# HGRN2 with keys taken into the exponential as logarithms, and a Newton step in two operations

## The chip, the core and the metric

One core of one Trainium2 chip runs the whole program. The metric is device time in microseconds (us), the median of the runs shown. The engines are TensorE (PE in the profile, with its weight loads as PEld), VectorE (DVE), ScalarE (ACT), GpSimd (POOL) and SyncE (SP), which issues most of the DMAs.

## The reference

A trunk of one layer on 1024 tokens of width 1024 in float32: a SwiGLU feed-forward part, a mixer of three branches (S5, HGRN2, RG-LRU), a second SwiGLU part and a final norm. The change concerns the second branch, which has four heads of 128 key and 128 value channels and works in chunks of 64 tokens:

```
qh = silu(q);  log_f = log(lb + (1 - lb) * sigmoid(zf));  kh = (1 - lb) * sigmoid(-zf)
# for each chunk, with the state from the chunk before
b = cumsum(log_f)
o_inter = (qc * exp(b)) @ state
scores[t, s] = sum_d qc[t, d] * exp(b[t, d] - b[s, d]) * kc[s, d]      for s <= t
o = o_inter + scores @ vc
state = exp(b_last) * state + (kc * exp(b_last - b)).T @ vc
# after the chunks, per head
out = o * rsqrt(mean(o * o) + 1e-6) * norm_w * silu(g)
```

## The kernel before

The products with weights, which are most of the work, run on TensorE in float32 by three passes over exact halves (`mm3`, lines 207 to 209). The mixers' elementwise work runs on the other engines beside them. `w_in` projects all columns; `pbuf_out` applies each column's first function, and for the f columns computes the key `k = (1 - lb) * sigmoid(-z)` on the way (lines 1501 to 1505); all goes to scratch in DRAM.

HGRN2 comes afterwards, in eight halves: four heads `j`, two halves `hf` of the tokens (512 columns). `run` (lines 1705 to 1708) calls `hgrn` for one half and then a few steps of the generator `fill`: the merges of the branches (`merge`: product, evacuation `th` on VectorE in line 1549, sums on GpSimd in line 1554) and the first half of the output product. The table `FILL` says how many steps. What an engine runs in which order is set by a list scheduler when the program is built; each engine's queue is then fixed and runs in order.

One half (`hgrn_half`), with channels on the partitions and tokens on the columns:

- A logarithm on ScalarE (line 1021) and a scan on VectorE (line 1024) give `b`, the running sum of log f in each chunk of 64. Two exponentials give `E = exp(b)` and `Ek = exp(b_last - b)`, whose difference GpSimd takes (lines 1027 to 1029).
- Level 64: VectorE multiplies queries with `E` and keys with `Ek` (lines 1035 to 1040) into `QK`, `Qin` and `Kh`. All elementwise products here go through the helper in line 1020, so the trace tells them apart by their tiles only.
- Six levels of block size H = 32 to 1 (lines 1057 to 1076). In each, GpSimd subtracts a reference from `b` for the two halves of the blocks into `Dl`, ScalarE takes the exponential in place, VectorE multiplies the key half with `k` and the query half with `q` (256 columns each), TensorE forms four 128 x 128 score products (line 1051), and VectorE copies them by mask into `sc`.
- The keys are transposed, the state is advanced, the outputs are summed in `po` (lines 1078 to 1102).
- The head norm: the sum of squares in `pm` by a product with ones (line 1106), then `rsqrt` (lines 223 to 235): logarithm and exponential on ScalarE and one Newton step of five operations on VectorE. Then `y` with the norm weight (line 1109), times the gate `g` on GpSimd.

Tiles of a half live in one of two tags, `h` with nine and `h2` with eight slots, for even and odd heads; a slot comes free when its last reader is done. `b`, `sc`, `Qin` and `Kh` keep theirs through the levels, `Dl` takes a new one in each level.

Of the kernel before, what the change touches and what calls it, by code (L numbers as in the profile page):

```python
# [11 lines left out]
ALU = mybir.AluOpType  # L12
# [27 lines left out]
def pack(inp):  # L40
    """small parameters, channel-major on 128 partitions (layout only)"""
# [20 lines left out]
class Trunk:  # L62
# [3 lines left out]
    COPIES = 3      # of four rounded on DVE  # L66
# [22 lines left out]
    def open_psum(self, **kinds):  # L89
        """eight banks in sets"""  # L90
        self.banks.close()
        self.pp = self.banks.enter_context(self.tc.tile_pool(name=self.nm("pp"), bufs=1, space=PSUM, reuse_waits="tile"))
        self.kinds = kinds

    def ps(self, kind="g"):
        """one PSUM bank of a set"""
        return self.pp.tile([P, HALF], F32, name=self.nm("ps"), tag="ps" + kind, bufs=self.kinds[kind])
# [4 lines left out]
    def open_pool(self, ctx, side="right", **bufs):  # L102
        """tags of equal slots; the tiles of one tag share its slots in program order"""
# [8 lines left out]
    # ---- constants  # L112
    def consts(self):
# [9 lines left out]
        nc.scalar.activation(out=warm, in_=self.epsb, func=AF.Sqrt)      # the table of the first norm  # L123
# [7 lines left out]
    # ---- weight stream: raw float32 tiles ahead of their exact hi/lo halves  # L131
    def add_unit(self, src, k, c=P, kind="n"):
        """src: AP [128, k, c], k * c <= 1024"""
        self.units.append((src, k, c, kind))

    def add_cols(self, w, c0, k0=0, k=KD, c=P, kind="n"):
        """rows [k0*128, (k0+k)*128) and columns [c0, c0+c) of w"""
# [22 lines left out]
    def _split_unit(self, i):  # L160
# [13 lines left out]
        if kind == "u":  # L174
            # weight sums of the seven products: A11, A12 from g, A21, A22 from u
# [13 lines left out]
    def after_unit(self, ahead):  # L189
        """queue the block's loads behind the load of the weights `ahead` units from here"""  # L190
# [11 lines left out]
    def mm3(self, ps, pairs, start=True, stop=True):  # L202
        """ps += sum of l.T @ r over the pairs, float32 by three passes over exact halves"""
# [18 lines left out]
    # ---- 1/sqrt(v) for v = scale * a + eps, polished by one Newton step  # L222
    def rsqrt(self, a, scale, table=None):
        nc = self.nc
        ln, v, r = (self.slot("t") for _ in range(3))
        b = nc.scalar.activation(out=ln, in_=a, func=AF.Ln, scale=scale, bias=self.epsb)
        if table is not None:
            self.order(b, table)
        nc.vector.tensor_scalar(out=v, in0=a, scalar1=scale, scalar2=EPS, op0=ALU.mult, op1=ALU.add)
        nc.scalar.activation(out=r, in_=ln, func=AF.Exp, scale=-0.5)  # L230
        nc.vector.tensor_tensor(out=ln, in0=r, in1=r, op=ALU.mult)
        nc.vector.tensor_tensor(out=v, in0=v, in1=ln, op=ALU.mult)
        nc.vector.tensor_scalar(out=v, in0=v, scalar1=-0.5, scalar2=1.5, op0=ALU.mult, op1=ALU.add)
        nc.vector.tensor_tensor(out=r, in0=r, in1=v, op=ALU.mult)
        return r

    def rsqrt_small(self, o, a, scale):
        """o = 1/sqrt(scale * a + eps) for a few values a partition"""
# [12 lines left out]
    def act_set(self, sid, after):  # L251
        """ask for an activation-table set once `after` have been issued"""
# [10 lines left out]
    # ---- the residual stream, tokens on partitions: tile (g, cq) holds tokens 256 g.. and columns 256 cq.. as [128, 2, 256]  # L263
# [3 lines left out]
    def stats(self, hf):  # L267
        """columns for the sums of squares of one half of the tokens: [128, 4 tiles, 4 parts]"""
# [8 lines left out]
    def inv_rms(self, sq, i0=0, i1=4, n=4):  # L277
        """1 / rms of the token tiles [i0, i1)"""
# [24 lines left out]
    # ---- FFN, first part: silu(h @ gate) * (h @ up), to scratch  # L303
    # The gate and up columns of one tile are the two rows of a 2 x 2 block product with the halves of the inner
    # dimension and of the tokens: seven block products in place of eight.
    def t_open(self, ctx):
        """slots for the halves of the seven blocks, before that for the tiles they come from"""
# [11 lines left out]
    def t_blocks(self, src, n, names, parts=1):  # L319
        """w * x of one half of the tokens, transposed, in float32 and as halves, in parts of the tokens;  # L320
        src(i, d): normed x [128 tokens, 128 columns]"""
# [16 lines left out]
    def t_second(self, src, n):  # L338
        """B12 serves only the tiles done in eight products"""
# [32 lines left out]
    def tiles8(self, hf, w, parts=1):  # L372
        """the first tiles of gate and up columns in eight products, a half of the tokens"""
# [24 lines left out]
    def tick(self):  # L398
        """work beside the products: one job is done and the loads of the next begin, every so many products"""
# [7 lines left out]
    def pair7(self, out, early=False):  # L407
        """two column tiles of a product with h, by seven products; out(column tile, half, its value)"""
# [10 lines left out]
        tt(g1, g0, p6)                                  # P1 + P6  # L419
        if not early:  # L420
            p2 = prod("g", w, 4, "21")
        tt(g0, g0, p2)                                  # P1 + P2
# [4 lines left out]
        tt(u0, g1, p7)                                  # P1 + P6 + P7  # L427
        tt(g1, g1, p5)                                  # P1 + P6 + P5
# [11 lines left out]
    def tile7(self, f, sums=False):  # L440
# [9 lines left out]
        tt(g1, g0, p6)                                  # P1 + P6  # L450
        p2 = prod("g", w, 4, "21")
        tt(g0, g0, p2)                                  # gate, first half: P1 + P2
# [4 lines left out]
        tt(u0, g1, p7)                                  # P1 + P6 + P7  # L457
# [1316 lines left out]
```

## Time and profile before

| | us |
|---|---|
| median of three runs | 2341.26 (2340.84 to 2343.86) |
| span of the profiled execution, first to last instruction | 2343.5 |
| run time nearest to that span | 2343.86 |
| TensorE busy | 2270.5 (97%) |
| TensorE weight loads busy | 1902.2 (81%) |
| VectorE busy | 1803.5 (77%) |
| ScalarE busy | 940.8 (40%) |
| GpSimd busy | 248.0 (11%) |

The profiled execution's own time is not marked among the runs; the nearest, 2343.86 us, is 0.36 us above the span. The busy shares are averages over stages with different limits, so they must be read stage by stage. Where the rows below speak of idle time before an instruction, they name the work that ended it. A busy TensorE is not one at its peak, since matmuls are pipelined and their ends are modelled.

### The profile page before, as it was taken

The page shows a single profiled execution, that of the slowest core. Times are in us where ns is not written, and L with a number is a line of the kernel's source. Part 1 is how long each engine was busy: PE and PEld are TensorE (multiplying, and loading weights), DVE is VectorE, ACT ScalarE, POOL GpSimd, SP SyncE. Part 2 cuts the span into 40 slices and gives each one's busy share as a digit, 9 for nine tenths or more (in the row PEclk, how much of TensorE's full clock was granted, in tenths as well). Part 3 has the DMA queues.
Part 4 walks back from the last instruction along what each step waited for, and adds up shares of the span by engine and source line. Part 5 has one row for each costly group of instructions (what it writes and reads, how often), then busy time and mean ns, then how long its engine had stood idle before and what let it go on. Part 6 is the DMA issues. An engine that isn't in the chain of part 4 may idle for free.

```text
span 2343.5 us, 32057 instructions
## 1 busy us (share of the span) xinstructions
PE 2270.5 (97%) x11476; PEld 1902.2 (81%) x11476; DVE 1803.5 (77%) x3179; ACT 940.8 (40%) x1510; POOL 248.0 (11%) x250
## 2 busy tenths in 40 slices
PE   7999999999999999999999998899999999999998
PEld 6788888899789888887778777788978888888887
DVE  6976777698797876667887989986478777775796
ACT  5323222222466523435665533344423222234455
POOL 0100000005200300000000445520020000000000
PEclk9999999999999999999999999999999999999999
DMA  5122433474843446563445543347513433348633
GB/s 154 57 87 86 116 113 121 147 249 122 272 158 124 135 142 202 180 196 108 148 137 148 174 143 125 104 141 228 158 32 119 151 104 117 102 136 288 215 95 117
DMA packets 354255, 336.96 MB, mean 144 GB/s; under 512 B 43920, under 2 KB 258320, under 8 KB 354080
## 3 DMA queue, kind: packets, MB, share of 16 engines
q1 hardware_dynamic: 353920, 334.36, 45.2%
q8 instruction: 90, 1.47, 0.3%
q0 software_dynamic: 176, 0.56, 0.1%
q14 instruction: 69, 0.57, 0.1%
HBM read 233.53 MB, written 102.50 MB: 143 GB/s over the span
## 4 chain that ended last, share of the span: by engine, by line
PE 78%; DVE 12%; DMA 3%; issue 3%; POOL 1%; ACT 1%; SPq 1%; DVEq 0%; ACTq 0%; POOLq 0%
PE ps L208 25%; PE ps L207 25%; PE ps L209 24%; DVE w L157 2%; DVE Dl L1020 1%; DVE th L1549 1%; DVE TT L317 1%; POOL tb L343 1%; PE ps L1051 1%; PE ps L292 1%; DVE S L177 1%; DMA yl<-y 1%; PE ps L905 0%; DVE b L1024 0%; DVE tb L343 0%
## 5 line engine op out<-in xcount | busy, mean ns | idle before, releaser
L208 PE MATMUL ps<-T,w 128*128 128x512 f32 (+1 forms) x992 | 384.2, 388 | 1.4 <-DVE T L317 1.4
L207 PE MATMUL ps<-T,w 128*128 128x512 f32 (+1 forms) x992 | 383.6, 389 | 1.2 <-DVE T L316 1.2
L209 PE MATMUL ps<-T,w 128*128 128x512 f32 (+1 forms) x992 | 380.7, 385 | 0.0
L156 ACT CAST w<-raw 128x1024 fp32r<-128x1024 f32 (+2 forms) x218 | 181.7, 836 | 357.5 <-PE ps L208 309.7
L157 DVE TENSOR_TENSOR w<-raw,w 128x1024 fp32r<-128x1024 f32 (+2 forms) x218 | 212.5, 976 | 66.5 <-ACT w L156 63.5
L156 ACT CAST w<-S 128x1024 fp32r<-128x1024 f32 x128 | 134.3, 1049 | 320.6 <-PE ps L208 318.5
L208 PE MATMUL ps<-TT,w 128*128 128x512 f32 x640 | 254.4, 398 | 7.0 <-DVE TT L317 6.9
L209 PE MATMUL ps<-TT,w 128*128 128x512 f32 x640 | 251.4, 393 | 0.0
L207 PE MATMUL ps<-TT,w 128*128 128x512 f32 x640 | 250.4, 394 | 0.0
L207 PEld LDWEIGHTS ps<-T,w 128*128 128x128 f32 x992 | 186.1, 189 | 43.3 <-DVE T L316 1.9
L208 PEld LDWEIGHTS ps<-T,w 128*128 128x128 f32 x992 | 187.0, 189 | 41.0 <-DVE T L317 2.2
L209 PEld LDWEIGHTS ps<-T,w 128*128 128x128 f32 x992 | 187.0, 189 | 39.3 <-DVE w L157 0.2
L445 DVE TENSOR_TENSOR g<-g,ps 128x512 f32<-128x512 f32 x160 | 109.9, 687 | 116.7 <-PE ps L209 115.6
L157 DVE TENSOR_TENSOR w<-S,w 128x1024 fp32r<-128x1024 f32 x128 | 161.3, 1261 | 22.7 <-ACT w L156 18.4
L208 PEld LDWEIGHTS ps<-TT,w 128*128 128x128 f32 x640 | 120.6, 188 | 38.7 <-DVE TT L317 12.5
L207 PEld LDWEIGHTS ps<-TT,w 128*128 128x128 f32 x640 | 121.0, 189 | 27.9
L208 PE MATMUL ps<-b,ah 128*128 128x512 f32 x360 | 142.3, 396 | 0.0
L209 PEld LDWEIGHTS ps<-TT,w 128*128 128x128 f32 x640 | 120.8, 189 | 26.4
L156 ACT CAST ah<-ar 128x512 fp32r<-128x512 f32 (+2 forms) x153 | 79.9, 524 | 150.8 <-PE ps L208 101.4
L207 PE MATMUL ps<-b,ah 128*128 128x512 f32 x360 | 137.9, 393 | 0.0
L209 PE MATMUL ps<-b,ah 128*128 128x512 f32 x360 | 134.0, 392 | 0.0
L157 DVE TENSOR_TENSOR ah<-ar,ah 128x512 fp32r<-128x512 f32 (+2 forms) x153 | 86.3, 571 | 46.7 <-ACT ah L156 42.9
(408 smaller groups left out, 5041.5 us busy)
## 6 DMA issues: line engine op xcount, KB each, us to landing
raw<-in_w_in_dram SPq DMA_DIRECT2D x56, 512.0 KB
raw<-in_ffn_gate_dram SPq DMA_DIRECT2D x44, 512.0 KB
raw<-in_ffn_up_dram SPq DMA_DIRECT2D x44, 512.0 KB
B<-in_ffn_down_dram SPq DMA_DIRECT2D x68, 256.0 KB
ar<-s SPq DMA_DIRECT2D x68, 256.0 KB
ar<-a SPq DMA_DIRECT2D x66, 256.0 KB
s<-S SPq DMA_DIRECT2D x62, 256.0 KB
a<-a SPq DMA_DIRECT2D x56, 256.0 KB
```

Of the source, the lines that this page charges most:

```text
L156: self.nc.scalar.copy(hi, src)
L157: self.last_lo = self.nc.vector.tensor_tensor(out=lo, in0=src, in1=hi, op=ALU.subtract)
L177: tt = lambda o, a, b, op: nc.vector.tensor_tensor(out=o, in0=a, in1=b, op=op)
L207: nc.tensor.matmul(out=ps, lhsT=lh, rhs=rh, start=start and j == 0, stop=False)
L208: nc.tensor.matmul(out=ps, lhsT=lh, rhs=rl, start=False, stop=False)
L209: self.last_mm = nc.tensor.matmul(out=ps, lhsT=ll, rhs=rh, start=False, stop=stop and j == n - 1)
L292: self.nc.tensor.transpose(ps[:, i * P:(i + 1) * P], src(i), self.ident)
L317: self.nc.vector.tensor_tensor(out=lo[:, c], in0=x[:, c], in1=hi[:, c], op=ALU.subtract)
L343: tt = lambda o, a, b, e=self.nc.vector: e.tensor_tensor(out=o, in0=a, in1=b, op=ALU.subtract)
L445: tt = lambda o, a, b, op=ALU.add: V.tensor_tensor(out=o, in0=a, in1=b, op=op)
L1020: tt = lambda o, a, b, op, e=V: e.tensor_tensor(out=o, in0=a, in1=b, op=op)
L1051: nc.tensor.matmul(out=ps[:, c * P:(c + 1) * P], lhsT=lh[:, c * P:(c + 1) * P], rhs=rh[:, c * P:(c + 1) * P], start=True, stop=True)
```

## The change

Every place where the key was multiplied with an exponential now has the key's logarithm inside that exponential: `c = b - ln k` is formed once per half, and the differences for the key side are taken against `c` in place of `b`, so that `exp(ref - c) = k * exp(ref - b)`. The exponential of `Ek` is written straight to its two users. `k` is held above 1e-37 so that its logarithm exists. The Newton step of the head norm uses `r * (r * r * (pm + P * eps) - 3 P)`, two fused operations on VectorE and a square on ScalarE, with the factor -0.5 / P moved into the norm weight.

```diff
@@ rsqrt(): removed
@@ hg_setup
+        self.hg_nwn = t("hg_nwn")
+        n0, n1 = COL["hg_nw"]
+        self.order(nc.vector.tensor_scalar(out=self.hg_nwn, in0=self.cp[:, n0:n1], scalar1=-0.5 / P, scalar2=None, op0=ALU.mult), self.last_lo)
@@ hgrn_half
         V.tensor_tensor_scan(out=b, data0=self.reset, data1=sz, initial=0.0, op0=ALU.mult, op1=ALU.add)
+        cc = self.slot(ht, name="c")
+        A.activation(out=cc, in_=k, func=AF.Ln)
+        tt(cc, b, cc, ALU.subtract)
         E, Ek = sz, self.slot(ht, name="Ek")
-        tt(Ek.rearrange("p (c i) -> p c i", i=64), b6[:, :, 63:64].to_broadcast([P, 8, 64]), b6, ALU.subtract, G)
+        tt(Ek.rearrange("p (c i) -> p c i", i=64), b6[:, :, 63:64].to_broadcast([P, 8, 64]), c6, ALU.subtract, G)
         A.activation(out=E, in_=b, func=AF.Exp)
-        A.activation(out=Ek, in_=Ek, func=AF.Exp)
-        tt(QK4[:, :, 0, :], k4[:, :, 0, :], ek4[:, :, 0, :], ALU.mult)
+        A.activation(out=QK4[:, :, 0, :], in_=ek4[:, :, 0, :], func=AF.Exp)
+        A.activation(out=Kh4[:, :, 1, :], in_=ek4[:, :, 1, :], func=AF.Exp)
         tt(QK4[:, :, 1, :], q4[:, :, 1, :], e4[:, :, 1, :], ALU.mult)
-        tt(Kh4[:, :, 1, :], k4[:, :, 1, :], ek4[:, :, 1, :], ALU.mult)
         for H in self.LEVELS:
-            tt(d4[:, :, 0, :], ref, bb[:, :, 0, :], ALU.subtract, G)
+            tt(d4[:, :, 0, :], ref, cb[:, :, 0, :], ALU.subtract, G)
             tt(d4[:, :, 1, :], bb[:, :, 1, :], ref, ALU.subtract, G)
             A.activation(out=Dl, in_=Dl, func=AF.Exp)
-            tt(QK4[:, :, 0, :], blk(k, H)[:, :, 0, :], d4[:, :, 0, :], ALU.mult)
             tt(QK4[:, :, 1, :], blk(q, H)[:, :, 1, :], d4[:, :, 1, :], ALU.mult)
-        r = self.rsqrt(pm, 1.0 / P)
+        r, r2 = self.slot("t"), self.slot("t")
+        A.activation(out=r, in_=pm, func=AF.Ln, scale=1.0 / P, bias=self.epsb)
+        A.activation(out=r, in_=r, func=AF.Exp, scale=-0.5)
+        A.activation(out=r2, in_=r, func=AF.Square)
+        V.scalar_tensor_tensor(out=r2, in0=pm, scalar=P * EPS, in1=r2, op0=ALU.add, op1=ALU.mult)
+        V.scalar_tensor_tensor(out=r, in0=r2, scalar=3.0 * P, in1=r, op0=ALU.subtract, op1=ALU.mult)
-        V.scalar_tensor_tensor(out=y, in0=po, scalar=self.col("hg_nw", j), in1=r, op0=ALU.mult, op1=ALU.mult)
+        V.scalar_tensor_tensor(out=y, in0=po, scalar=self.hg_nwn[:, j:j + 1], in1=r, op0=ALU.mult, op1=ALU.mult)
@@ pbuf_out
-                self.nc.vector.tensor_scalar(out=k, in0=k, scalar1=self.omlb[:, j:j + 1], scalar2=None, op0=ALU.mult)
+                self.nc.vector.tensor_scalar(out=k, in0=k, scalar1=self.omlb[:, j:j + 1], scalar2=1e-37, op0=ALU.mult, op1=ALU.max)
```

The scheduler makes a new order for the stage; outside it the queues keep theirs. In the changed program the line numbers are smaller by 3 to 15: line 1020 is 1008 there, 1051 is 1042, 1074 and 1076 are 1064 and 1066, 1109 is 1105, 1549 is 1546.

VectorE, in the levels of the first two halves (tiles 125.. to 126.. belong to the first, 127.. to 128.. to the second; `sc` is the scores' tile, `ps` a PSUM bank). Before:

```order
L1020 TENSOR_TENSOR Dl_12644<-k_12558,Dl_12644 128x128x2
L1020 TENSOR_TENSOR Dl_12644<-q_12560,Dl_12644 128x128x2
L1020 TENSOR_TENSOR Dl_12866<-k_12792,Dl_12866 128x64x4
L1020 TENSOR_TENSOR Dl_12866<-q_12794,Dl_12866 128x64x4
L1076 COPY_PREDICATED sc_12582<-mask_1572,ps_12614 128x16x16
L1076 COPY_PREDICATED sc_12816<-mask_1565,ps_12836 128x8x32
L1020 TENSOR_TENSOR Dl_12656<-k_12558,Dl_12656 128x256
L1020 TENSOR_TENSOR Dl_12656<-q_12560,Dl_12656 128x256
L1076 COPY_PREDICATED sc_12582<-mask_1579,ps_12626 128x32x8
L1020 TENSOR_TENSOR Dl_12878<-k_12792,Dl_12878 128x128x2
L1020 TENSOR_TENSOR Dl_12878<-q_12794,Dl_12878 128x128x2
L1076 COPY_PREDICATED sc_12816<-mask_1572,ps_12848 128x16x16
```

and now:

```order
L1008 TENSOR_TENSOR Dl_12633<-q_12562,Dl_12633 128x64x4
L1066 COPY_PREDICATED sc_12586<-mask_1572,ps_12616 128x16x16
L1008 TENSOR_TENSOR Dl_12849<-q_12789,Dl_12849 128x32x8
L1066 COPY_PREDICATED sc_12586<-mask_1579,ps_12627 128x32x8
L1066 COPY_PREDICATED sc_12813<-mask_1565,ps_12832 128x8x32
L1008 TENSOR_TENSOR Dl_12644<-q_12562,Dl_12644 128x128x2
L1008 TENSOR_TENSOR Dl_12655<-q_12562,Dl_12655 128x256
L1066 COPY_PREDICATED sc_12586<-mask_1586,ps_12638 128x64x4
L1066 COPY_PREDICATED sc_12813<-mask_1572,ps_12843 128x16x16
L1008 TENSOR_TENSOR Dl_12860<-q_12789,Dl_12860 128x64x4
```

Each level has one multiply in place of two, and the masked copies of earlier levels stand closer behind.

VectorE, in the head norm of the first half (`s` are the norm's tiles, line 229 to 234 the old Newton step, `w` a weight half for TensorE). Before:

```order
L229 TENSOR_SCALAR s_12701<-ps_12698 128x512
L231 TENSOR_TENSOR s_12700<-s_12702 128x512
L1549 SCALAR_TENSOR_TENSOR th_13188<-th_13188,ps_13190 128x512
L232 TENSOR_TENSOR s_12701<-s_12701,s_12700 128x512
L233 TENSOR_SCALAR s_12701<-s_12701 128x512
L229 TENSOR_SCALAR s_12935<-ps_12932 128x512
L234 TENSOR_TENSOR s_12702<-s_12702,s_12701 128x512
L231 TENSOR_TENSOR s_12934<-s_12936 128x512
L1109 SCALAR_TENSOR_TENSOR y_12710<-ps_12676,cp,s_12702 128x512
L1024 SCALAR_TENSOR_TENSOR b_13033<-reset_12266,f_13024 128x512
```

and now:

```order
L1546 SCALAR_TENSOR_TENSOR th_12980<-th_12980,ps_12982 128x512
L1102 SCALAR_TENSOR_TENSOR s_12699<-ps_12696,s_12699 128x512
L1546 SCALAR_TENSOR_TENSOR th_12996<-th_12996,ps_12998 128x512
L1103 SCALAR_TENSOR_TENSOR s_12698<-s_12699,s_12698 128x512
L157 TENSOR_TENSOR w_13202<-raw_12940,w_13201 128x512
L1105 SCALAR_TENSOR_TENSOR y_12705<-ps_12674,hg_nwn,s_12698 128x512
L1012 SCALAR_TENSOR_TENSOR b_13021<-reset_12268,f_13012 128x512
L1008 TENSOR_TENSOR c_13023<-b_13021,c_13023 128x512
```

Five operations are two, and the subtraction for `c` stands behind the scan of the next half.

TensorE, in the first levels of the same halves (lines 207 to 209 are the products of `merge` between; `x4` four products). Before:

```order
L1051 MATMUL ps_12602<-Dl_12596 128x128 x4
L207 MATMUL ps_12956<-yh_12335,w_12752 128x512
L208 MATMUL ps_12956<-yl_12336,w_12752 128x512
L209 MATMUL ps_12956<-yh_12335,w_12753 128x512
L207 MATMUL ps_12956<-yh_12363,w_12752 128x512
L1051 MATMUL ps_12614<-Dl_12608 128x128 x4
L1051 MATMUL ps_12626<-Dl_12620 128x128 x4
L1051 MATMUL ps_12836<-Dl_12830 128x128 x4
L1051 MATMUL ps_12848<-Dl_12842 128x128 x4
```

and now:

```order
L1042 MATMUL ps_12605<-Dl_12600 128x128 x4
L207 MATMUL ps_12944<-yh_12337,w_12747 128x512
L208 MATMUL ps_12944<-yl_12338,w_12747 128x512
L1042 MATMUL ps_12616<-Dl_12611 128x128 x4
L1042 MATMUL ps_12627<-Dl_12622 128x128 x4
L1042 MATMUL ps_12832<-Dl_12827 128x128 x4
L209 MATMUL ps_12944<-yh_12337,w_12748 128x512
L207 MATMUL ps_12944<-yh_12365,w_12747 128x512
L208 MATMUL ps_12944<-yl_12366,w_12747 128x512
L1042 MATMUL ps_12843<-Dl_12838 128x128 x3
L1042 MATMUL ps_12638<-Dl_12633 128x128 x4
L1042 MATMUL ps_12843<-Dl_12838 128x128
```

The levels follow each other with fewer products of `merge` between them.

## Rows read from the trace of the kernel before

**Rows 1.** The page, busy tenths in 40 equal slices of the span, three engines.

```profile
PE   7999999999999999999999998899999999999998
...
DVE  6976777698797876667887989986478777775796
...
POOL 0100000005200300000000445520020000000000
```

**Rows 2.** Busy time by stretches: us, then each engine, granted clock, DMA, GB/s.

```profile
1320.00:1560.00 240.00, 211.16 (x1237) 178.01 (x1235) 223.04 (x378) 90.44 (x154) 128.50 (x134) 0.98 0.38 122
1320.00:1330.00 10.00, 7.51 (x28) 5.59 (x27) 10.00 (x14) 5.38 (x10) 7.80 (x8) 0.83 0.28 88
1360.00:1370.00 10.00, 10.00 (x59) 8.44 (x59) 4.31 (x10) 2.13 (x4) 0.00 (x0) 1.00 0.24 80
1460.00:1470.00 10.00, 6.17 (x42) 5.27 (x42) 10.00 (x17) 3.79 (x8) 8.41 (x10) 1.00 0.58 174
1470.00:1480.00 10.00, 9.35 (x49) 8.61 (x50) 8.73 (x18) 2.26 (x5) 5.26 (x7) 0.66 0.19 65
```

**Rows 3.** Waits of TensorE, 1320 to 1560: total us, times, longest.

```profile
PE ps L207 <- DVE th L1549: 9.4, 8, 2.1
PE ps L1051 <- DVE Dl L1020: 8.7, 8, 2.6
PE ps L1080 <- DVE sc L1076: 2.2, 2, 1.2
PE ps L1051 <- DVE QK L1020: 1.7, 1, 1.7
...
PE ps L207 <- ACT yh L218: 0.3, 1, 0.3
```

**Rows 4.** VectorE groups by form, 1300 to 1600: busy us, mean ns, idle before.

```profile
L1020 DVE TENSOR_TENSOR Dl<-k,Dl 128x256 f32<-128x256 f32 x48 | 28.9, 602 | 0.0
...
L1549 DVE SCALAR_TENSOR_TENSOR th<-th,ps 128x512 f32<-128x512 f32 x40 | 27.2, 679 | 6.1 <-PE ps L209 6.1
...
L232 DVE TENSOR_TENSOR s<-s,s 128x512 f32<-128x512 f32 x8 | 6.9, 861 | 0.1
...
L234 DVE TENSOR_TENSOR s<-s,s 128x512 f32<-128x512 f32 x8 | 6.3, 789 | 0.1
...
L229 DVE TENSOR_SCALAR s<-ps 128x512 f32<-128x512 f32 x8 | 5.6, 694 | 1.6 <-ACT s L226 1.6
...
L231 DVE TENSOR_TENSOR s<-s 128x512 f32<-128x512 f32 x8 | 5.4, 681 | 0.0
...
L1020 DVE TENSOR_TENSOR Kh<-k,Ek 128x256 f32<-128x256 f32 x8 | 5.4, 675 | 0.0
...
L1020 DVE TENSOR_TENSOR QK<-k,Ek 128x256 f32<-128x256 f32 x8 | 4.7, 583 | 0.0
...
L233 DVE TENSOR_SCALAR s<-s 128x512 f32<-128x512 f32 x8 | 3.9, 482 | 0.1
```

**Rows 5.** ScalarE groups by form, 1300 to 1600.

```profile
L1021 ACT ACTIVATE f<-f,hg_lb,hg_omlb 128x512 f32<-128x512 f32 x8 | 6.4, 812 | 17.7 <-DMA f<-pf 17.7
L275 ACT ACTIVATE junk<-x 128x256 f32<-128x256 f32 x14 | 5.7, 408 | 13.6 <-DVE x L1575 13.6
...
L230 ACT ACTIVATE s<-s 128x512 f32<-128x512 f32 x8 | 5.0, 631 | 0.2
```

**Rows 6.** Waits of GpSimd on other work, 1320 to 1560.

```profile
POOL Dl L1020 <- DVE Kh L1020: 6.3, 4, 3.7
POOL Dl L1020 <- DVE Dl L1020: 4.3, 2, 2.2
```

**Rows 7.** GpSimd groups by form, 1300 to 1600, the costliest.

```profile
L1020 POOL TENSOR_TENSOR Dl<-b 128x256 f32<-128x256 f32 x96 | 77.7, 838 | 13.0 <-DVE Kh L1020 6.3 <-DVE Dl L1020 4.3 <-PE ps L1051 1.7
```

**Rows 8.** Tile Dl: ns min/median/max, first and last start.

```profile
L1020 POOL TENSOR_TENSOR Dl<-b x96: 606/800/1941, 1325.9 to 1539.7; 128x256 f32<-128x256 f32 x96
...
L1020 DVE TENSOR_TENSOR Dl<-k,Dl x48: 405/420/1490, 1335.1 to 1546.3; 128x256 f32<-128x256 f32 x48
```

More of the change, by code (lines that the diff above doesn't have):

```diff
@@ L220, in split @@
         return hi, lo
[L223 to L235, printed above, removed]
     def rsqrt_small(self, o, a, scale):
@@ L1024, in hgrn_half @@
         V.tensor_tensor_scan(out=b, data0=self.reset, data1=sz, initial=0.0, op0=ALU.mult, op1=ALU.add)
+        cc = self.slot(ht, name="c")
+        A.activation(out=cc, in_=k, func=AF.Ln)
+        tt(cc, b, cc, ALU.subtract)
         E, Ek = sz, self.slot(ht, name="Ek")
-        b6 = b.rearrange("p (c i) -> p c i", i=64)
-        tt(Ek.rearrange("p (c i) -> p c i", i=64), b6[:, :, 63:64].to_broadcast([P, 8, 64]), b6, ALU.subtract, G)
+        b6, c6 = (t.rearrange("p (c i) -> p c i", i=64) for t in (b, cc))
+        tt(Ek.rearrange("p (c i) -> p c i", i=64), b6[:, :, 63:64].to_broadcast([P, 8, 64]), c6, ALU.subtract, G)
         A.activation(out=E, in_=b, func=AF.Exp)
-        A.activation(out=Ek, in_=Ek, func=AF.Exp)
         blk = lambda t, H: t.rearrange("p (n h i) -> p n h i", h=2, i=H)
         QK, Qin, Kh = self.slot(ht, name="QK"), self.slot(ht, name="Qin"), self.slot(ht, name="Kh")
-        e4, ek4, q4, k4, QK4, Qin4, Kh4 = (blk(t, 64) for t in (E, Ek, q, k, QK, Qin, Kh))
+        e4, ek4, q4, QK4, Qin4, Kh4 = (blk(t, 64) for t in (E, Ek, q, QK, Qin, Kh))
         d1, d2 = e4[:, :, 0, 63:64], e4[:, :, 1, 63:64]
-        tt(QK4[:, :, 0, :], k4[:, :, 0, :], ek4[:, :, 0, :], ALU.mult)
+        A.activation(out=QK4[:, :, 0, :], in_=ek4[:, :, 0, :], func=AF.Exp)
+        A.activation(out=Kh4[:, :, 1, :], in_=ek4[:, :, 1, :], func=AF.Exp)
         tt(QK4[:, :, 1, :], q4[:, :, 1, :], e4[:, :, 1, :], ALU.mult)
@@ L1058, in hgrn_half @@
             n = HALF // (2 * H)
-            bb = blk(b, H)
+            bb, cb = blk(b, H), blk(cc, H)
             Dl = QK = self.slot(ht, name="Dl")
```

## The prediction

> **What bounds the kernel now.** I began with the busy tenths of the page [rows 1]. TensorE is full almost everywhere. Counted from 0, a slice is 58.6 us; in the slices 24 and 25 (1406 to 1523 us) it sinks to 8, and in 22 to 25 VectorE is at 8 to 9 and GpSimd, idle for most of the program, at 4 to 5. That is the HGRN2 stage, the only place that the change touches apart from set-up and the clamp in the f columns. The table by stretches [rows 2] then gives the stage in numbers: from 1320 to 1560 us TensorE is busy for 211.16 of 240 us, VectorE for 223.04, ScalarE for 90.44 and GpSimd for 128.50. Inside, VectorE is full in one ten-microsecond stretch (1320) and leaves TensorE at 7.51; where VectorE is at 4.31 (1360), TensorE is full. So VectorE bounds this stage. TensorE loses 240 - 211.16 = 28.8 us there, and a little more by its clock: the granted clock is 0.83 in the stretch at 1320 and 0.66 in that at 1470, the first of which holds idle time of TensorE while the second follows a stretch in which it was busy for only 6.17, against 1.00 in the other two. That is 10 x 0.17 + 10 x 0.34 = 5.1 us. TensorE's own work is thus about 240 - 28.8 - 5.1 = 206 us.
>
> Third I read who TensorE waits for in the stage [rows 3]. The ten causes add up to 28.4 us, nearly all of them VectorE. They fall into two kinds. **Queue waits**, where VectorE is late because other work is ahead: the evacuation `th` 9.4 us, and the masked copies into `sc` (2.2, and 1.2 and 1.0 among the lines left out): 13.8 us. **Chain waits**, where a GpSimd, a ScalarE and a VectorE step follow each other for a level: `Dl` 8.7, `QK` 1.7, ScalarE's `s` and `Dl`, and three small ones: 14.6 us.
>
> **The change part by part.** *Taken from VectorE*, by the rows of its groups [rows 4], for all eight halves: the key multiplies of the six levels 28.9 us (48 of 602 ns), the two of level 64, 4.7 and 5.4, and the five operations of the old Newton step 5.6 + 5.4 + 6.9 + 3.9 + 6.3 = 28.1. Sum 67.1 us. (One half's norm lies at the end of the stage or just past it; I leave it in.)
>
> *Put on VectorE*, per half: the subtraction that makes `c` (both inputs in SBUF, 512 columns) and two fused Newton operations. None is in the trace. For `c` and the second Newton operation the nearest row is L234, also two SBUF inputs of that size: 789 ns; the ends are 681 (L231) and 861 (L232). The first Newton operation reads one input from PSUM like L1549: 679 ns. So 8 x (0.789 + 0.789 + 0.679) = 18.1 us, between 16.3 and 19.2. Net VectorE loses 67.1 - 18.1 = 49 us and comes to 223 - 49 = 174 us, well below TensorE's 206. The order shows the same: ten rows fewer a half.
>
> *Put on ScalarE*, per half: a logarithm of `k`, a square, and the exponential of `Ek` cut into two of 256 columns. The square is like L230 (631 ns), the logarithm between that and L1021 (812, which has two operands by partition); I take 631. A 256-column activation is at 408 (L275), so the cut adds 2 x 0.408 - 0.631 = 0.19 us [rows 5]. That is 8 x 1.45 = 11.6 us. ScalarE was idle for 150 of the 240 us, and this goes there; where the cover is gone, 11.6 us is the most it could cost.
>
> *GpSimd*: as many instructions as before; the key half only reads `c` where it read `b`. *TensorE* and the DMAs: the same number of instructions. *The start of a half gets longer*: `c` must wait for the scan and lie behind it on VectorE, and `Ek` on GpSimd waits for `c`. For later halves this is done a half ahead and costs nothing; for the first pair, where nothing is ahead, GpSimd starts two such subtractions later, 2 x 0.8 = 1.6 us, and I take 2. *One more slot*: `c` holds one of the nine or eight slots of its tag up to the last level. GpSimd already waits for slots a little ([rows 6]: 4.3 us for those of earlier levels, 6.3 us for that of `Ek`); I cost it at nothing here, since one of the two multiplies that a level's slot waits for is gone, and keep it for a rival. The clamp to 1e-37 rides on an existing operation, the scaled norm weight is one operation of four columns at start-up, under full TensorE: nothing.
>
> *What comes back.* With VectorE at 174 against TensorE's 206 the queue waits go: 13.8 us. Of the chain waits half stay, since VectorE is only one of three links and GpSimd's 838 ns a subtraction [rows 7] remain: 7.3 us. Of the clock loss, half: 2.5. Less the longer start, 2. Sum 13.8 + 7.3 + 2.5 - 2 = 21.6, taken as **21 us**. What is late next is TensorE itself. The profiled execution would go from 2343.5 to 2322.5 us; it lies 2.2 us above the median of the runs, 2341.26, so the forecast is **2320 us**.
>
> *A rule that speaks against one part.* VectorE's square of `r`, L231, takes 681 ns and ScalarE's 631 for the same size [rows 4, 5]. The Trainium skill ("ScalarE: Activation LUTs", Rules for kernel authors) wants multiplications on VectorE, which it calls up to three times faster per element in bf16. By it the moved square would save nothing; here, in float32, the rows show no such lead, and the square leaves the fuller engine, so the sum above keeps its 5.4 us.
>
> **The rivals.** *Everything comes back* (2309 us). Both kinds of wait and the clock go, less the start: 28.8 + 5.1 - 2 = 32 us. For it: the 256-column multiply takes 405 ns at its least and 602 on average, GpSimd's subtraction 606 at its least and 838 on average [rows 4, 7, 8]; while both run each is slow, so fewer multiplies may also give GpSimd up to 96 x 0.232 = 22 us, and the chains shorten. Against it: the new order packs the halves more densely between the other products, so that VectorE stays at some 85% of TensorE's time, in queues of fixed order. The Trainium skill ("SBUF — State Buffer", Who interferes with whom) states that a VectorE instruction with two SBUF inputs and a GpSimd instruction that reads SBUF lock each other out; the two pairs of durations agree with it, and by it this rival is the likelier.
>
> *GpSimd and the chain set the pace* (2331 us). GpSimd is at 128.50 of 240 us overall, but at 7.80 and 8.41 of 10 in the stretches at 1320 and 1460, where TensorE loses most. If all chain waits stay and the clock loss with them, only the queue waits are won, less the start and a us or two of new waits: 13.8 - 2 - 2 = 10 us.
>
> *No change that can be told* (2339 us). Faster by 2 us only: the tighter order packs until VectorE is full again, and the queue waits come back. Against it: 49 of 223 us is more than the new order can pack away, as TensorE's work per half is the same.
>
> *Slower* (2362 us). The slot of `c` decides. The tag with eight slots holds `b`, `c`, `sc`, `Qin` and `Kh` through the levels and leaves three for `Dl`, where four were. A slot comes free only when TensorE has done the scores of an earlier level, and TensorE runs its queue in order with other products between. If every one of the 24 levels of that tag then stalled GpSimd by the longest wait seen for a level's slot, 2.2 us [rows 6], and TensorE behind it, that is 53 us, less the 32 to be won: 21 us slower. It decides from 32/24 = 1.3 us a level on. Against it: GpSimd runs ahead of TensorE here, and such a wait came twice in the whole stage; those for `Ek`'s slot end with a multiply that the change removes.
>
> **How the numbers follow.** I give the forecast 0.55 (own range 2314 to 2327: half or all of the chain waits stay, and the bounds of the new operations), everything back 0.17, the chain's pace 0.20, no change 0.05, slower 0.03. A measurement of this kernel tells about 0.2%, 4.7 us, from no change. Faster by more than that: 0.55 + 0.17 + 0.20 = 0.92; the same 0.05; slower 0.03. The range reaches from 2309 to 2333: it leaves out about half of "everything back", a third of "the chain's pace" and the last two, some 0.2 in all.
>
> **What would show it.** In the changed profile, VectorE's busy time over the stage should be near 174 us and that of TensorE above 95% of it; the waits of TensorE for `th` should be gone and those for `Dl` about halved; the stage should end some 20 us earlier, with nothing changed before 1320 us and the same work behind. GpSimd's mean subtraction should sink below 838 ns. The prediction is wrong if TensorE still waits for `th`, if GpSimd's waits for a slot grow into tens of us, or if the time changes in another stage.

## The result, and the profile after

The changed kernel takes 2319.39 us (median of 4 runs, 2319.25 to 2319.55), the kernel before in the same session 2342.56 us (2340.84 to 2346.44): a ratio of 0.9895, 95% interval 0.9882 to 0.9908. It is faster by 23 us; the forecast was 2320.

Line numbers in this section are those of the changed program. The page's busy tenths in 40 slices, to set beside [rows 1]:

```profile
PE   7999999999999999999999999999999999999998
...
DVE  6886777698798766667888888866488777775796
...
POOL 0200000005200300000000265710020000000000
```

TensorE's two eights are gone, and VectorE has gone down in the slices 22 and 24 to 26. The stage itself, as in [rows 2]; its last sum of squares lies at 1537.3 us, where before it lay at 1566.8. Of these 29.5 us, 6.6 come back right behind it (76.1 us now, 69.5 before, up to the second mark below), so the marks, and not this instruction, measure the stage:

```profile
1316.20:1537.10 220.90, 207.11 (x1248) 177.23 (x1247) 185.88 (x304) 100.01 (x178) 128.90 (x135) 0.99 0.42 134
...
1376.00:1386.00 10.00, 8.35 (x54) 7.05 (x53) 10.00 (x16) 4.35 (x8) 9.12 (x10) 1.00 0.22 74
...
1446.00:1456.00 10.00, 9.43 (x66) 8.76 (x67) 7.34 (x16) 3.61 (x6) 7.24 (x9) 1.00 0.32 109
...
1486.00:1496.00 10.00, 8.26 (x48) 7.06 (x46) 10.00 (x14) 4.53 (x9) 8.49 (x8) 1.00 0.31 105
1496.00:1506.00 10.00, 9.50 (x40) 7.88 (x41) 9.85 (x16) 4.31 (x9) 5.23 (x4) 0.83 0.22 69
```

TensorE is busy for 94% of it, VectorE for 84% (93% before). What TensorE still loses lies mostly in stretches like those at 1376 and 1486, where VectorE is full and GpSimd nearly so: VectorE has room on average, but not there. Who TensorE waits for from 1310 to 1537 us, beside [rows 3]:

```profile
PE ps L1042 <- DVE Dl L1008: 5.1, 9, 1.7
PE ps L207 <- DVE th L1546: 4.5, 2, 2.2
PE ps L1042 <- ACT Dl L1056: 0.9, 1, 0.9
PE ps L1070 <- DVE sc L1066: 0.8, 2, 0.6
...
PE ps L1042 <- DVE sc L1066: 0.3, 1, 0.3
```

With four small ones left out these are 13.3 us, where 28.4 us stood. VectorE's groups (1280 to 1620 us), beside [rows 4]:

```profile
L1008 DVE TENSOR_TENSOR Dl<-q,Dl 128x256 f32<-128x256 f32 x48 | 31.5, 662 | 20.2 <-ACT Dl L1056 20.0
...
L1008 DVE TENSOR_TENSOR c<-b,c 128x512 f32<-128x512 f32 x8 | 7.8, 983 | 0.1
...
L1103 DVE SCALAR_TENSOR_TENSOR s<-s,s 128x512 f32<-128x512 f32 x8 | 6.2, 773 | 0.1
...
L1102 DVE SCALAR_TENSOR_TENSOR s<-ps,s 128x512 f32<-128x512 f32 x8 | 5.5, 684 | 3.5 <-ACT s L1101 3.5
```

VectorE now idles for 20.0 us before its multiply because it waits for ScalarE's exponential; it has changed from the one that others wait for into one that waits. ScalarE's new operations (beside [rows 5]) and GpSimd's subtractions (beside [rows 7]), 1310 to 1540 us:

```profile
L1101 ACT ACTIVATE s<-s 128x512 f32<-128x512 f32 x8 | 5.0, 629 | 0.2
...
L1015 ACT ACTIVATE c<-k 128x512 f32<-128x512 f32 x8 | 4.9, 620 | 0.0
...
L1026 ACT ACTIVATE QK<-Ek 128x256 f32<-128x256 f32 x8 | 3.3, 417 | 16.7 <-POOL Ek L1008 16.7
L1027 ACT ACTIVATE Kh<-Ek 128x256 f32<-128x256 f32 x8 | 3.2, 402 | 0.0
```

```profile
L1008 POOL TENSOR_TENSOR Dl<-b,c 128x256 f32<-128x256 f32 x48 | 40.8, 849 | 9.4 <-PE ps L1042 9.4
L1008 POOL TENSOR_TENSOR Dl<-b 128x256 f32<-128x256 f32 x48 | 37.8, 787 | 0.0
```

**Where the 23 us lie.** Two marks fence the stage in every version: the last `g<-g,ps` of the projection ahead of it and the first `y<-ps,cp` of the part behind it (last and first start in these rows of the two lines).

```profile
L412 DVE TENSOR_TENSOR g<-g,ps x96: 664/686/690, 794.3 to 1294.2; 128x512 f32<-128x512 f32 x96
...
L331 ACT ACTIVATE y<-ps,cp x16: 667/686/728, 1636.3 to 1709.0; 128x512 f32<-128x512 f32 x16
```

Those are of the kernel before; of the changed one:

```profile
L397 DVE TENSOR_TENSOR g<-g,ps x96: 660/685/690, 792.6 to 1290.3; 128x512 f32<-128x512 f32 x96
...
L316 ACT ACTIVATE y<-ps,cp x16: 669/689/731, 1613.4 to 1685.5; 128x512 f32<-128x512 f32 x16
```

Between the marks 342.1 us have become 323.1, so 19.0 of the 25.8 us between the two spans (2343.5 and 2317.7) lie in the stage. 3.9 us lie ahead of it and 2.9 behind it, where the queues are the same. A second profile of the changed kernel has the first mark at 1293.3, 3.0 us later than the first profile, with 325.1 us between the marks. So 17 to 19 us are the change's own, and the stretch ahead of the stage, which it does not touch, differs by 3 us between executions of one program. Behind the stage the versions below take either 704.3 to 704.7 us or 706.9 to 707.3; `red_ahead`, as fast as the changed kernel, is among the latter, so those 2.9 us are not tied to the change either.

### The profile page after: what moved, and what is told of

Same layout as the page of the kernel before. It is cut to its first block, busy times and chain, and to the rows that moved or that the text cites. A ratio compares the mean times of both kernels' runs of the same rounds, so it can differ in the third digit from the quotient of the medians.

```text
span 2317.7 us, 32005 instructions
## 1 busy us (share of the span) xinstructions
PE 2258.5 (97%) x11476; PEld 1899.0 (82%) x11476; DVE 1763.0 (76%) x3100; ACT 950.3 (41%) x1534; POOL 247.0 (11%) x250
## 4 chain that ended last, share of the span: by engine, by line
PE 41%; DVE 5%; issue 2%; POOL 2%; ACT 1%; DMA 1%; SPq 0%; DVEq 0%; ACTq 0%; POOLq 0%
PE ps L208 13%; PE ps L207 13%; PE ps L209 13%; POOL Dl L1008 1%; DVE w L157 1%; PE ps L1042 1%; DVE th L1546 0%; DMA f<-pf 0%; PE ps L890 0%; DVE TT L302 0%; DMA yl<-y 0%; DVE b L1012 0%; POOL Ek L1008 0%; SPq L815 0%; DMA th<-p 0%
## 5 line engine op out<-in xcount | busy, mean ns | idle before, releaser
L208 PEld LDWEIGHTS ps<-TT,w 128*128 128x128 f32 x640 | 120.8, 189 | 39.0 <-DVE TT L302 12.8
L157 DVE TENSOR_TENSOR ah<-ar,ah 128x512 fp32r<-128x512 f32 (+2 forms) x153 | 85.9, 568 | 44.2 <-ACT ah L156 40.5
```

Source lines behind the costliest of these rows:

```text
L157: self.last_lo = self.nc.vector.tensor_tensor(out=lo, in0=src, in1=hi, op=ALU.subtract)
L208: nc.tensor.matmul(out=ps, lhsT=lh, rhs=rl, start=False, stop=False)
```

## The experiments

All versions have the changed kernel's text but for edits whose main lines are shown; each gets a new order from the scheduler, and that alone may move the stage by a few us (`slot_less`, with the same instructions, moved it by 3.3). The theory: VectorE's total work bounded the stage, and the time falls with it until some slack is reached. Rivals: the chain of GpSimd, ScalarE and VectorE for one level sets the pace; GpSimd, freed from VectorE's multiplies, becomes faster; slots.

**The two parts alone.** `keys_only` has the old five-operation Newton step back, `newton_only` the old key multiplies:

```diff
 keys_only
-        A.activation(out=r2, in_=r, func=AF.Square)
...
+        r = self.rsqrt(pm, 1.0 / P)
 newton_only
-        tt(cc, b, cc, ALU.subtract)
...
+            tt(QK4[:, :, 0, :], blk(k, H)[:, :, 0, :], d4[:, :, 0, :], ALU.mult)
```

> The key logarithms alone, with the old Newton step. VectorE loses 39.0 us of key multiplies and gains 7.8 us for c, so it should be about 31 us below the kernel before in the stage. Theory (VectorE's load sets the stage, whatever is taken off it): the gain follows the microseconds removed, 31 of 48 of the 23 us, so about 15 us and 2327 us. Rival A (the gain comes from GpSimd, which the two-input key multiplies blocked): nearly all of it, about 2322 us, with GpSimd's subtraction well below 838 ns. Rival B (the gain comes from the shorter chain of a level, which loses one of its two multiplies): all of it, about 2320 us.

> The new Newton step alone, with the old keys. VectorE loses 28.1 us and gains 11.7. Theory: 16 of 48 parts of the gain, about 8 us, 2335 us. Rival A: the norm's operations lie mostly apart from GpSimd's subtractions, 2 to 4 us, about 2339 us. Rival B: the levels are unchanged, 0 to 2 us, about 2341 us.

Measured: the keys alone 2333.14 us, ratio 0.9948 (0.9932 to 0.9963), 327.6 us between the marks; the Newton step alone 2334.14 us, 0.9957 (0.9941 to 0.9973), 336.4 us. In the stage they win 14.5 and 5.7 us, together 20.2 against 17.0 and 19.0 for both at once; but the profiled execution of `keys_only`, 2327.95 us, is 5 us faster than its three others. By the medians they win 10.7 and 9.7 us, together 20.4 against 23.2. The Newton step came out as the theory had it (2335), the keys 6 us slower than it had (2327) and still further from both rivals. The parts add up within this scatter; shares of one load would, and two causes side by side would too.

**VectorE's load put back with one-input work.** `dummy_red` adds 64 reductions of 256 columns, 8 in each half: 48 in the levels, 16 at level 64.

```diff
...
+            V.tensor_reduce(out=self.junk[:, 0:1], in_=blk(q, H)[:, :, 0, :], op=ALU.add, axis=mybir.AxisListType.XY)
```

> The changed kernel with 64 added reductions on VectorE over 256 columns (one a level, two at level 64 of each half), which read q or E q's input and write one column that nobody reads: about 64 x 0.4 = 26 us of VectorE time that is in no chain and has one SBUF input. It computes the same output. Theory: 26 of the 48 us are back, so 12 us of the gain go and the time is about 2331 us, with TensorE's waits for the evacuation th back. Rival A: an operation with one input does not block GpSimd, so about 2321 us. Rival B: no chain is longer, so about 2321 us.

Measured: 2331.7 us, 0.9946 (0.9930 to 0.9961), 331.1 us between the marks: 8.0 more than the changed kernel, and the time that the theory gave. But 4.6 of these lie before the first logarithm of the stage, where twelve of the reductions stand ahead of it, and 3.0 are a wait: a filler had been given an input that came late by DMA, and VectorE's queue stood behind it. The groups of the reductions, in the levels and at level 64, and the instruction that waited:

```profile
L1061 DVE TENSOR_REDUCE hjunk<-q 128x1 f32<-128x256 f32 x48 | 20.1, 418 | 0.3
...
L1034 DVE TENSOR_REDUCE hjunk<-q 128x1 f32<-128x256 f32 x16 | 6.6, 413 | 3.1 <-DMA q<-pq 3.0
```

```profile
1303.00 0.42 DVE L1034 TENSOR_REDUCE hjunk<-q 128x1 f32<-128x256 f32 x1 [3.01 <-DMA q<-pq]
```

So 26.7 us of added operations cost between 3.4 us (less all 4.6) and 5.0 us (less the 3.0 of the wait) of the stage as load. The other 4.8 of the 12.8 us between the two spans lie outside the marks. With a filler that brought a wait of its own, the run does not settle the matter.

**The old key multiplies put back in part.** `old3` has them in the levels 32, 16 and 8, `old5` in 32 to 2:

```diff
 old5
-            tt(d4[:, :, 0, :], ref, cb[:, :, 0, :], ALU.subtract, G)
+            tt(d4[:, :, 0, :], ref, (bb if H in (32, 16, 8, 4, 2) else cb)[:, :, 0, :], ALU.subtract, G)
...
+            if H in (32, 16, 8, 4, 2):
+                tt(QK4[:, :, 0, :], blk(k, H)[:, :, 0, :], d4[:, :, 0, :], ALU.mult)
```

> The changed kernel with the key multiplies back in the levels 32, 16 and 8 (24 operations of some 0.6 us, 14 to 15 us of VectorE); c stays. Theory: 14.5 of 48 parts of the gain go, 7 us, about 2326 us. Rival A: about the same, 2327 us, with GpSimd's subtraction slower. Rival B: half of the gain goes, about 2331 us.

> The changed kernel with the key multiplies back in the same five levels (40 operations with two SBUF inputs, 24 to 32 us); c, the two exponentials of level 64 and the new Newton step stay. Theory 1: 24 to 32 us of load, 10 to 14 us slower than the changed kernel. Theory 2: like the reductions ahead, 7 to 12 us slower. Theory 3: clearly more than the reductions ahead, by 5 us and over, with GpSimd's subtractions longer than there.

Measured: `old3` 2329.2 us, 0.9932 (0.9914 to 0.9950), 333.3 us between the marks; `old5` 2328.57 us, 0.9926 (0.9912 to 0.9941), 333.2 us. Both cost 8 to 10 us, though `old5` adds 26.1 us of multiplies and `old3` only 19.7, at 819 ns each. `old3` lies between its theory (2326) and rival B (2331). `old5` is 8.3 us above the changed kernel beside it (`after_again`, below), less than theory 1 had. That is more than 5 us above `red_ahead`, as theory 3 had it, but GpSimd's subtractions, 801 ns on average, are not longer than there (820), as it also wanted. The multiplies of `old3`, then of `old5`:

```profile
L1008 DVE TENSOR_TENSOR Dl<-k,Dl 128x256 f32<-128x256 f32 x24 | 19.7, 819 | 0.6 <-ACT Dl L1056 0.6
...
L1008 DVE TENSOR_TENSOR Dl<-k,Dl 128x256 f32<-128x256 f32 x40 | 26.1, 652 | 1.2 <-ACT Dl L1056 1.2
```

**The same places with reductions that wait for nothing new.** `red_ahead` puts 40 reductions of the level's own `Dl` where those 40 multiplies stood, ahead of the query multiply and so in the chain; `red_behind` puts them behind it; `after_again` is the changed kernel once more, on the same chip.

```diff
 red_ahead
...
+            rd = V.tensor_reduce(out=self.junk[:, 0:1], in_=d4[:, :, 0, :], op=ALU.add, axis=mybir.AxisListType.XY) if H in (32, 16, 8, 4, 2) else None
+            qm = tt(QK4[:, :, 1, :], blk(q, H)[:, :, 1, :], d4[:, :, 1, :], ALU.mult)
...
+                self.order(qm, rd)
```

> The same 40 reductions, but of the key half of Dl and ordered ahead of the query multiply, where the key multiply stood: the same load, now in the chain of the level. The output is unchanged. Theory 1: the same as behind, 5 to 8 us slower than the changed kernel. Theory 2: 7 to 10 us slower, clearly more than behind. Theory 3: 0 to 2 us slower, as the operation has one SBUF input.

> The changed kernel with one reduction of 256 columns on VectorE in each of the five levels 32 to 2 of each half (40 in all, some 17 us), which reads the query half of Dl after its multiply and therefore stands behind it: it loads VectorE but lies in no chain to TensorE. The output is unchanged. Theory 1 (the load alone counts): 17 us of the 48 removed, at the 0.3 to 0.5 us of time for a us of load that the single parts gave, so 5 to 8 us slower than the changed kernel. Theory 2 (the length of a level's chain counts): 0 to 2 us slower. Theory 3 (the lock with GpSimd counts): 0 to 2 us slower.

> The changed kernel once more, so that the next three have it beside them on one chip: 2319 to 2322 us. Every theory expects the same of it.

Measured: `red_ahead` 2320.04 us, 0.9890 (0.9873 to 0.9908), 320.9 us between the marks; `red_behind` 2324.38 us, 0.9909 (0.9891 to 0.9927), 322.4 us; `after_again` 2320.31 us, 0.9893 (0.9876 to 0.9911), 325.1 us. Forty more steps of VectorE in the chain of a level cost nothing that can be told, as theory 3 had it. That speaks against the chain's pace, and leaves open why multiplies at the same places cost 8 us. As a test of load it is weak: the query multiplies took 572 ns here and 662 in the changed kernel, so VectorE's busy time rose by 6.9 us only. The runs of `red_behind` (2321.43 to 2328.21 us) overlap those of `after_again` (2318.53 to 2324.47), so its 4 us decide between no theories.

**A second operand, and nothing else.** `max_ahead` puts the maximum of `Dl` with itself there: two operands from SBUF as the multiply has them, and unchanged values.

```diff
+            if H in (32, 16, 8, 4, 2):
+                tt(d4[:, :, 0, :], d4[:, :, 0, :], d4[:, :, 0, :], ALU.max)
```

> The changed kernel with 40 maxima of the level's key exponent with itself, in place, in the levels 32 to 2, put where the key multiply of the kernel before stood: VectorE reads two operands there, as that multiply did, but the values stay as they are. The forty one-input reductions at the same place took 410 ns each and cost nothing (2320.0 us); the forty key multiplies took 652 ns each and cost some 8 us (2328.6 us). Theory 1, the second operand decides (it makes VectorE and GpSimd get in each other's way): about 650 ns each, VectorE some 200 to 206 us busy in the stage, and 2325 to 2330 us. Theory 2, the extra step in the chain or the mere load decides: about 410 ns each and 2319 to 2322 us, as with the reductions.

Measured: 2329.5 us, 0.9945 (0.9928 to 0.9962), 332.9 us between the marks, and 680 ns each, as theory 1 had it: the second operand decides, and the mere step in the chain does not. (The maximum also writes 256 columns where the reduction writes one; against that as the cause, the evacuation `th` of the changed kernel, which writes 512 but reads only one operand from SBUF, takes 0.68 us without GpSimd and 0.67 beside it.) The groups of `max_ahead`, 1310 to 1540 us:

```profile
L1008 DVE TENSOR_TENSOR Dl<-q,Dl 128x256 f32<-128x256 f32 x48 | 33.9, 708 | 0.3 <-ACT Dl L1056 0.3
L1008 DVE TENSOR_TENSOR Dl<-Dl 128x256 f32<-128x256 f32 x40 | 27.2, 680 | 2.1 <-ACT Dl L1056 2.0
```

and of `red_ahead`:

```profile
L1009 DVE TENSOR_TENSOR Dl<-q,Dl 128x256 f32<-128x256 f32 x48 | 27.4, 572 | 2.2 <-ACT Dl L1057 2.1
...
L1058 DVE TENSOR_REDUCE hjunk<-Dl 128x1 f32<-128x256 f32 x40 | 16.4, 410 | 5.9 <-ACT Dl L1057 5.9
```

The timeline of `max_ahead` (start, duration) shows what a second operand meets. First GpSimd, then VectorE:

```profile
1327.10 0.67 POOL L1008 TENSOR_TENSOR Dl<-b,c 128x256 f32<-128x256 f32 x1
1327.73 0.85 POOL L1008 TENSOR_TENSOR Dl<-b 128x256 f32<-128x256 f32 x1
...
1341.87 0.79 POOL L1008 TENSOR_TENSOR Dl<-b 128x256 f32<-128x256 f32 x1
1346.13 0.86 POOL L1008 TENSOR_TENSOR Dl<-b,c 128x256 f32<-128x256 f32 x1 [3.47 <-PE ps L1042]
```

```profile
1327.19 0.87 DVE L1008 TENSOR_TENSOR Dl<-Dl 128x256 f32<-128x256 f32 x1
...
1344.52 0.41 DVE L1008 TENSOR_TENSOR Dl<-Dl 128x256 f32<-128x256 f32 x1
1344.86 0.41 DVE L1008 TENSOR_TENSOR Dl<-q,Dl 128x256 f32<-128x256 f32 x1
```

At 1327 us GpSimd subtracts beside it and the maximum takes 0.87 us; from 1342.66 to 1346.13 GpSimd waits, and it takes 0.41. Over the timeline, 12 maxima with GpSimd idle take 0.41 us on average, 22 that lie wholly beside its work 0.82, and the other six, partly beside it, 0.69. The reductions of `red_ahead` do not care: 9 without GpSimd and 30 beside it both take 0.41 us. The Trainium skill ("SBUF — State Buffer", Who interferes with whom) says that VectorE with two SBUF inputs contends with a GpSimd instruction that reads SBUF, and that `tensor_reduce` does not; these runs agree with both.

**Slots, the square, and GpSimd's share.** `slot_less` takes one slot from each of the two tags; `sq_dve` moves the square of `r` back to VectorE; `sub_dve` moves 16 of GpSimd's 96 subtractions to VectorE.

```diff
 slot_less
-                    self.open_pool(S, h=9, h2=8, w=1)
+                    self.open_pool(S, h=8, h2=7, w=1)
 sq_dve
-        A.activation(out=r2, in_=r, func=AF.Square)
+        tt(r2, r, r, ALU.mult)
 sub_dve
-            tt(d4[:, :, 1, :], bb[:, :, 1, :], ref, ALU.subtract, G)
+            tt(d4[:, :, 1, :], bb[:, :, 1, :], ref, ALU.subtract, V if H <= 2 else G)
```

> The changed kernel with one buffer less for each of the two sizes of work tiles (8 and 7 in place of 9 and 8). Tests the rival that the slots which the logarithm of the keys holds take room from the exponents: by it GpSimd and VectorE wait for a free buffer, GpSimd's waits before its subtractions grow above their 9.4 us, and the time is 2325 to 2345 us. If the slots have room to spare, 2318 to 2322 us.

> The changed kernel with the square of the head norm on VectorE again, eight operations. ScalarE falls by 8 x 0.63 = 5.0 us, VectorE rises by 8 x about 0.68 = 5.4 us in the stage. If VectorE has some 16 us of slack after the change, as the reductions say, 2318 to 2322 us; if every us of VectorE is paid for, 2325 us; if ScalarE were the tighter one by now, 2315 us.

> The changed kernel with the subtraction of the query half of the levels 2 and 1 moved from GpSimd to VectorE, sixteen operations: GpSimd falls by 16 x 0.82 = 13 us, VectorE rises by 16 x about 0.62 = 10 us. If GpSimd's pace holds the exponents back now (the changed kernel's remaining waits of TensorE for them are 5 to 6 us), 2314 to 2318 us; if VectorE's slack is used up by operations that read two operands beside GpSimd, as with the key multiplies, 2322 to 2327 us; if neither, 2319 to 2321 us.

Measured: `slot_less` 2316.66 us, 0.9889 (0.9874 to 0.9904), 319.8 us between the marks. GpSimd does wait longer for slots, 21.8 us in place of 9.4, and the time does not rise:

```profile
POOL Dl L1008 <- PE ps L1042: 18.2, 13, 4.2
...
POOL Dl L1008 <- DVE Dl L1008: 3.6, 1, 3.6
```

So the rival of the slots falls: with one slot less than the change left, nothing is lost. Its median is the shortest of all, 2.7 us under the changed kernel's, but the two intervals overlap, so it can't be told from it.

`sq_dve`: 2324.24 us, 0.9920 (0.9905 to 0.9935), 326.5 us between the marks, 1.4 and 3.4 more than the two profiles of the changed kernel. The interval overlaps that of the changed kernel, and its runs spread from 2320.59 to 2326.48. Its median lies nearest to the 2325 us of "every us is paid for"; what it shows is only that the square gains nothing on VectorE, where it took 813 ns. `sub_dve`: 2320.41 us, 0.9903 (0.9888 to 0.9917), 323.0 us. VectorE took 16 more operations of 738 ns, GpSimd was relieved of as many, and the time stayed, as expected if neither is the limit. GpSimd's pace then does not hold the stage, unless a gain there and a loss on VectorE just cancelled.

**All versions in one row each.** VectorE's busy time is that of the whole program, from the page; the stage is the time between the marks, and the last column what TensorE stands idle in it, all in us. Each row is one execution.

| version | VectorE busy | stage | TensorE idle |
|---|---|---|---|
| before | 1803.5 | 342.1 | 31.4 |
| newton_only | 1792.2 | 336.4 | 28.5 |
| max_ahead | 1790.0 | 332.9 | 27.8 |
| old5 | 1787.6 | 333.2 | 24.0 |
| dummy_red | 1784.6 | 331.1 (3.0 of it the wait for a DMA) | 23.8 |
| old3 | 1780.2 | 333.3 | 27.7 |
| keys_only | 1779.1 | 327.6 | 22.1 |
| red_behind | 1774.9 | 322.4 | 17.2 |
| sub_dve | 1772.7 | 323.0 | 17.8 |
| sq_dve | 1772.0 | 326.5 | 20.6 |
| red_ahead | 1769.9 | 320.9 | 15.0 |
| slot_less | 1766.9 | 319.8 | 16.2 |
| after_again, after | 1764.3, 1763.0 | 325.1, 323.1 | 18.5, 17.4 |

Up to about 1775 us the stage does not care, and stays between 320 and 327. Beyond, it grows by (342.1 - 322.4) / (1803.5 - 1774.9) = 0.7 us for each us of VectorE by its two ends; in between, from 1779 to 1790 us, the versions lie between 327.6 and 333.3 in no order. Part of the scatter is TensorE's clock, which loses 0 us in the stage of `max_ahead`, 6.8 in that of `old5`, 5.1 before, 1.7 and 3.4 in the two profiles of the changed kernel. The idle time leaves it out and shows the same knee, with (31.4 - 17.2) / (1803.5 - 1774.9) = 0.5 us for each us. The changed kernel stands some 12 us below that knee. Nearly all load above it has two operands in SBUF; the one version there with one-operand work, `dummy_red`, cost less in the stage, so how much is load as such and how much the second operand is not separated. `old3` lies 7 us above this line; its multiplies are all in the first levels, where GpSimd works beside them (819 ns each), and TensorE's waits for `Dl` are 11.1 us there. Whether that or its order is the reason was not tried.

## Why the prediction was right, point by point

- **VectorE bounds the stage: shown in the main.** VectorE's time put back took gain back, down to a knee below which it costs nothing that can be told; above the knee that was shown with two-operand work, and with one-operand work only by the flawed `dummy_red`. TensorE came to 94% of the stage; above 95% was expected.
- **VectorE would fall by 49 us, to 174: the size failed.** Over the whole program it fell by 1803.5 - 1763.0 = 40.5 us, between the marks by 39.6 (291.0 to 251.5), and in the stage's window it stands at 185.9. The step that failed is the subtraction of row durations from busy time. VectorE's instructions overlap: in the timeline above two that take 0.41 us start 0.34 us apart. The durations of all its instructions, summed, fall by 51.6 us (1989.5 to 1937.9), near the forecast 49; the engine is relieved of less, since 2242 neighbouring pairs overlapped by 187.1 us before and 2133 by 176.0 now, which is the 11.1 us between 51.6 and 40.5. Of the new operations only `c` was mis-sized, 983 ns for 789, above the upper end of 861: two of the eight ran with GpSimd idle and took 0.68 us, the other six, which read their two SBUF operands wholly or partly beside it, 1.08 on average. The Newton operations took 684 and 773.
- **The waits for `th` would go: half right.** 4.5 of 9.4 us stay, and of the queue waits as a whole 5.6 of 13.8 (`th` 4.5, `sc` 0.8 and 0.3): 8.2 us came back, not 13.8. The step that failed is from the average to the wait: VectorE has slack on average, but full stretches remain. The prediction had named "TensorE still waits for `th`" as a sign of being wrong, and another, a changed time in other stages; both are there, 4.5 us in two waits and 6.8 us outside the marks.
- **Half of the chain waits stay: right.** 7.7 of 14.6 us stay (13.3 less 5.6), so 6.9 came back, against 7.3.
- **Half of the clock loss: a little more.** Of all ten-microsecond stretches of the stage only that at 1496 us has a granted clock below 1.00, at 0.83, part of it at 1.2 in place of 2.4 GHz, behind the stretch at 1486 in which TensorE was busy for 8.26 us: 10 x 0.17 = 1.7 us are lost where 5.1 were, so 3.4 came back, against 2.5. The second profile loses 3.4 us and so gives back 1.7; this is most of the 2.0 us by which its stage is longer.
- **A longer start, 2 us: wrong in sign.** From the stage's first logarithm to the first score product of a level took 18.2 us before (1319.1 to 1337.3) and 15.9 us now (1315.3 to 1331.2). `c` is in the chain, but the key multiplies of level 64 no longer are.
- **The sum.** 8.2 + 6.9 + 3.4 = 18.5 us, where the stage won 19.0 and, by the second profile, 17.0; forecast 21.6. TensorE's idle time between the marks fell by 31.4 - 17.4 = 14.0, beside 8.2 + 6.9 by the waits. The too large queue term and the start's false cost partly cancelled. The medians differ by 23.2 us; the 4 to 6 us beyond the stage are in stretches that vary by 3 us between profiles, and why the medians share them stays open. That the median came within 1 us of the forecast is thus luck in part: the stage gave some 3 to 5 us less than forecast, and the rest came from elsewhere.
- **GpSimd's subtraction would sink below 838 ns: it did not.** It averages 818 (849 and 787), and its total is 247.0 against 248.0. The rival "everything comes back" rested on that. The trace does show the difference, but the change removed too little: 78 of the 96 subtractions still lie beside some VectorE operation with two SBUF operands (93 before) and take 0.85 us on average, the other 18 take 0.70. VectorE's operations change far more, as `max_ahead` shows.
- **The chain sets the pace: falls** by `red_ahead` and `sub_dve`. **The slot of `c`: falls** by `slot_less`. The rule that multiplications belong on VectorE (the Trainium skill, "ScalarE: Activation LUTs", Rules for kernel authors) finds nothing for it in these float32 runs: the square takes 629 ns on ScalarE and 813 on VectorE in `sq_dve`, which was not faster.

## What to carry to other kernels

Taking work from an engine that bounds a stage pays only until the next limit is reached: here some 0.5 to 0.7 us for each us down to the knee, and nothing that can be told for the last 12. Operations with two SBUF inputs are the ones to remove from VectorE while GpSimd reads SBUF; a one-input operation in the same place cost nothing that could be told. And durations of rows must not be subtracted from an engine's busy time one for one, since neighbours overlap.

## What the runs showed of the hardware

The size of the interference: in `max_ahead` a VectorE operation of 256 float32 columns with two SBUF operands took 0.41 us on average with GpSimd idle and 0.82 us wholly beside its work, even where both operands are the same tile. The query multiplies, with two different tiles, took 0.41 to 0.43 us with GpSimd idle in every version, and between 0.60 (`red_ahead`) and 1.05 (`old5`) on average wholly beside it. A reduction took 0.41 us either way in `red_ahead`, and the evacuation `th`, which has one operand in PSUM, 0.68 and 0.67 in the changed kernel. GpSimd's own subtraction moved less: 0.70 us without a two-operand operation of VectorE beside it and 0.85 with one in the changed kernel, and on average 801 ns in `old5`, 818 in the changed kernel and 848 in `max_ahead`.
